# Stick-breaking decoder trunk: compression weights in another pool, and VectorE's branch-d chain in parts behind weight splits

## The chip, the cores and the metric

The kernel runs on one core of a Trainium2 chip. The metric is the device time of one execution in microseconds; smaller is better. Five engines work beside each other, each through its own instructions in their order: TensorE (PE, with its weight loads as PEld), VectorE (DVE), ScalarE (ACT), GpSimd (POOL) and SyncE (SP), which here issues nearly all DMA transfers.

## The reference

Two layers (DEPTH 2) of a trunk with four causal token mixers, for 512 tokens of width 1024, in float32. Each layer normalises x, projects it by one matrix `w_in`, mixes in four branches and merges them through per-channel gates:

```
h = rmsnorm(x, norm_g[l])
c = split_columns(h @ w_in[l])
y_a = dilated_window_attention(...)          # 3 patterns, ALiBi
y_b = mla_attention(...)                     # low-rank q and kv
y_c = nsa_attention(... w1, b1, w2, b2 ...)  # compressed blocks, selected blocks, window
y_d = stick_breaking_attention(...)
merged = sum_i sigmoid(h @ w_merge[l, i] + b_merge[l, i]) * ((y_i * silu(gate_i)) @ w_branch[l, i])
x = x + merged @ w_out[l]
```

The two pieces that the change touches are the compression of branch c and the chain of branch d:

```
# compression: 31 blocks of 32 tokens, two stacks (keys, values)
hid = gelu(blocks.reshape(B, n_cmp, NSA_CMP_BLOCK * Dk) @ w1 + b1)
return hid @ w2 + b2
# stick breaking, per head and 128 queries
log1m = where(mask, log_sigmoid(-z), 0)
after = cumsum(log1m, reverse=True) - log1m
a = where(mask, exp(log_sigmoid(z) + after), 0)
out = a @ v
```

## The kernel before

**Weight chunks.** Nearly all of TensorE's work is products of the activations with weight chunks of 128 columns (`[P, 8, P]`, 512 KB; merge chunks take 2 rows of blocks more, 640 KB). A product in full float32 precision is made of three matmuls of reduced precision on split operands, high times high, high times low and low times high (`mm3`, L189 to L191, each 128x512). `split_chunk` (L234) loads a chunk on SP's queue into a `stage` tile (3 buffers) and splits it into a high and a low tile of the pool `w5`, which has 4 buffers, so that two chunks fit. The split is shared: of the first 5 row blocks of 128 (`W_SHARE`) ScalarE makes the high half (L175) and VectorE the low one (L176); of the other 3 (5 in a merge chunk) GpSimd makes both (L100, L185). A matmul of L191 needs the low tile, one of L189 the high one.

**Order.** A scheduler of the language puts the instructions of all stages in order from a timeline of its own and from priorities. `tc.high_priority` lets branches A, D and C begin before the weight work that stands ahead of them in the code, so that TensorE has products to do while the vector engines work on an attention. `after(a, b, why)` (L310) lays a dependence: instruction b does not start before a is done.

**Around the change.** In each layer the tail of branch A runs beside the compression and merge chunk (0,1). A's pairs go in units of two heads: scores (L290), VectorE's sum with the bias (L300), ScalarE's exponential (L302), VectorE's reciprocal (L303), GpSimd's normalisation (L305), TensorE's transposes (L325), ScalarE's copy (L327), TensorE's product with v (L331). The compression (`compress`, L584) projects keys and values, takes four tiles of `w1` (512 KB each, `[P, 8, P]`) through `stage` tiles and makes eight small matmuls (L629) with each, then gelu (L636 to L651).

Branch d (L724 to L759) goes in two pairs of heads. A pair has scores (L737) less a mask (L738) in three parts: two x tiles of 128x1024 and one `su` tile of 128x512. Then the minimum with 30 (L740), ScalarE's exponential (L741) and logarithm (L744), and on VectorE, for each part, the maximum (L746), scans (L751) and a subtraction (L752), with ScalarE's exponential behind (L753); then transposes and products with v. The chunks that are multiplied beside pair 0 are merge chunks, then the two chunks of `c_q` (`q_chunk`; low tiles w_448 and w_453); beside pair 1 those of the merge, of `c_gate` (`gate_chunks`, whose last step on VectorE is L568) and of the next merge. Layer 1 repeats layer 0, 545 us later. Line numbers are those of the kernel before.

Of the kernel before, what the change touches and what calls it, by code (L numbers as in the profile page):

```python
# [10 lines left out]
F32 = mybir.dt.float32  # L11
F32R = mybir.dt.float32r
AF = mybir.ActivationFunctionType
OP = mybir.AluOpType
PSUM = bass.MemoryType.PSUM

P = 128
# [28 lines left out]
W_SHARE = 5  # L46
# [40 lines left out]
def hybrid_trunk(ctx: ExitStack, tc: tile.TileContext, x, norm_g, w_in, mla_q_norm, mla_w_uq, mla_kv_norm,  # L87
# [3 lines left out]
    V, A, G, T = nc.vector, nc.scalar, nc.gpsimd, nc.tensor  # L91
# [16 lines left out]
    def s4(shape, dt=F32):  # L108
        return mk(sb, shape, dt, "s4", N_S4)
# [22 lines left out]
    def stage(shape):  # L132
        return mk(wp, shape, F32, "stage", 3)
# [38 lines left out]
    def split(hi, lo, src, scale=None):  # L172

        if scale is None:
            A.activation(hi, src, AF.Copy)  # L175
            V.tensor_tensor(lo, src, hi.bitcast(F32), op=OP.subtract)  # L176
        else:
            A.activation(hi, src, AF.Copy, scale=scale)
            V.scalar_tensor_tensor(lo, src, scale, hi.bitcast(F32), op0=OP.mult, op1=OP.subtract)

    def shared_split(hi, lo, src, a):

        split(hi[:, :a], lo[:, :a], src[:, :a])
        pool_copy(hi[:, a:], src[:, a:])
        G.tensor_tensor(lo[:, a:], src[:, a:], hi[:, a:].bitcast(F32), op=OP.subtract)  # L185

    def mm3(acc, sh, sl, mh, ml, start, stop):

# [42 lines left out]
    def wview(w, r0, rows, c0, cols):  # L231
        return w[r0:r0 + rows, c0:c0 + cols].rearrange("(k p) c -> p k c", p=P)

    def split_chunk(parts, nk):  # L234

        st = stage([P, nk, P])
        for k0, k1, c0, c1, ap in parts:
            nc.sync.dma_start(st[:, k0:k1, c0:c1], ap)
        hi, lo = w5([P, nk, P], F32R), w5([P, nk, P], F32R)
        shared_split(hi, lo, st, W_SHARE)  # L240
        return hi, lo

    def in_chunk(l, c0):
# [127 lines left out]
    def merge_chunks(l, plan, ys, am, mT):  # L371
        for cp, i in plan:
            first = cp not in am
            if first:
                am[cp] = [s4([P, 2, S]), 0]
            acc, am[cp][1] = am[cp][0], am[cp][1] + 1
            last = am[cp][1] == 4
            if last:
                mT[cp] = [(x4 if cp < 2 else s4)([P, 2, S], F32R) for _ in range(2)]
            for j in range(2):  # L380
                c = 2 * cp + j
                w = split_chunk([(0, KD, 0, P, wview(w_merge[l, i], 0, D, P * c, P)),
                                 (KD, KD + 2, 0, P, wview(w_branch[l, i], 0, 256, P * c, P))], KD + 2)
                pg = ps_d()
                proj_T(w, pg)
                th = th_tile()
                A.activation(th, pg, AF.Tanh, scale=0.5, bias=bmT[l][:, 8 * i + c:8 * i + c + 1])  # L387
                pb = ps_d()
                for k in range(2):
                    mm3(pb, w[0][:, KD + k], w[1][:, KD + k], ys[i][0][:, k], ys[i][1][:, k], k == 0, k == 1)  # L390
                if first:
                    V.scalar_tensor_tensor(acc[:, j], th, 1.0, pb, op0=OP.add, op1=OP.mult)
                else:
                    V.scalar_tensor_tensor(th, th, 1.0, pb, op0=OP.add, op1=OP.mult)  # L394
                    G.tensor_tensor(acc[:, j], acc[:, j], th, op=OP.add)  # L395
                if last:
                    split(mT[cp][0][:, j], mT[cp][1][:, j], acc[:, j], scale=0.5)
# [45 lines left out]
    for l in range(DEPTH):  # L443
# [140 lines left out]
        def compress():  # L584
# [37 lines left out]
            acc = ps_d()  # L622
            for s_ in range(2):
                for hf in range(2):
                    w1 = stage([P, 8, P])
                    nc.sync.dma_start(w1, nsa_w1[l, s_, 1024 * hf:1024 * hf + 1024].rearrange("(q p) c -> p q c", p=P))
                    for q in range(8 * hf, 8 * hf + 8):
                        g = 32 * (q % 4)
                        T.matmul(acc[g:g + 32, s_ * P:(s_ + 1) * P], blocks[s_][:, q], w1[:, q % 8], start=q < 4,  # L629
                                 stop=q >= 12, skip_group_check=True)  # L630
# [76 lines left out]
        merge_chunks(l, ((0, 1),), y, am, mT)  # L707
        gd = gate_chunks("d_gate")
        ks, kw, kc, vbd = compress()
        merge_chunks(l, ((1, 0),), y, am, mT)  # L710
        c_q = [q_chunk("c_q", c, cscale[:, c:c + 1]) for c in range(2)]

# [3 lines left out]
        cgv = cg.rearrange("p t (h j) -> p t h j", j=3)  # L716

        mark_c = tc.cur_priority
        merge_chunks(l, ((1, 1),), y, am, mT)
        gc = gate_chunks("c_gate")  # L720
        merge_chunks(l, ((0, 0),), y, am, mT)
# [2 lines left out]
        with tc.high_priority(offset=tc.cur_priority - mark):  # L724
            y[3] = new_y()
            for pr in range(2):
                ze = [(x4([P, 2, 512]), x4([P, 2, 512]), unit_tile().rearrange("p (h c) -> p h c", h=2)) for _ in range(2)]
                place = ((1, 384, 512), (2, 0, 256), (1, 0, 384), (0, 0, 512))

                def part(i, qt, h):  # L730
                    j, c0, c1 = place[qt]
                    return ze[i][j][:, h, c0:c1]

                for qt in (3, 2, 0, 1):
                    w = (qt + 1) * P
                    for h in range(2):
                        s = qk_unit(stacked(d_q[pr], d_k[pr][h], h), qt, w)  # L737
                        V.tensor_tensor(part(0, qt, h), s[:, :w], mask_tab[:, S + 1 - w:], op=OP.subtract)  # L738
                for j in range(3):
                    V.tensor_scalar(ze[1][j], ze[0][j], 30.0, None, op0=OP.min)  # L740
                    ex = A.activation(ze[1][j], ze[1][j], AF.Exp)  # L741
                with tc.issue_after(ex.ins):
                    for j in range(3):
                        A.activation(ze[1][j], ze[1][j], AF.Ln, bias=1.0)  # L744
                for j in range(3):
                    V.tensor_tensor(ze[1][j], ze[0][j], ze[1][j], op=OP.max)  # L746
                    for qt in range(NT):
                        if place[qt][0] == j:
                            for h in range(2):
                                er = part(1, qt, h)[:, ::-1]  # L750
                                V.tensor_tensor_scan(er, er, er, 0.0, op0=OP.add, op1=OP.bypass)  # L751
                    V.tensor_tensor(ze[0][j], ze[0][j], ze[1][j], op=OP.subtract)  # L752
                    A.activation(ze[0][j], ze[0][j], AF.Exp)  # L753
                acc = ps_o()
                for qts in ((3,), (2,), (0, 1)):
                    pv_cluster([([part(0, qt, h) for h in range(2)], qt,
                                 lambda h, kb: v_ad[1][:, kb, (2 * pr + h) * 64:(2 * pr + h + 1) * 64], False, True)
                                for qt in qts], acc)
                d_done = finish_pair(acc, gd, y[3], pr)  # L759
# [129 lines left out]
```

## Time and profile before

| | us |
|---|---|
| median of 3 runs | 1110.68 (1110.3 to 1111.24) |
| the profiled execution | 1114.14 |
| its span | 1112.4 |
| TensorE busy | 1078.8 (97%) |
| TensorE weight loads busy | 861.7 (77%) |
| VectorE, ScalarE, GpSimd busy | 541.5, 441.2, 464.4 |

Busy times are over the span. In the profile, a group line gives count, busy time and mean, and behind the last bar the idle time of the engine ahead of its instructions with what ended it. A timeline line gives start, duration, engine, line, operation, destination and sources, count, and in brackets the idle time before. A line with x12 is twelve instructions in a row. Matmuls overlap in the pipe, so the distance of two starts tells more than a duration. For the small matmuls (L331, L629) the trace has two records for each one of the program.

### The profile page before, as it was taken

To read this page: it belongs to the slowest core of one execution; us is meant where nothing else is said; L and a number is where in the kernel's file an instruction comes from. 1 tells how busy PE (TensorE), PEld (TensorE's weight loads), DVE (VectorE), ACT (ScalarE), POOL (GpSimd) and SP (SyncE) were. 2 spreads that over 40 slices of the span, in tenths; PEclk is the share of its full clock that TensorE was granted. 3 is DMA by queue.
4 is the path that set the end of the run, shared out by engine and by line. 5 is a ranking of instruction groups with operands and counts; after the bars stand their busy time and mean duration, and the time that the engine had idled before them with its cause. 6 is when DMAs were issued, how large, how long until landed. Compare 5 with 4: busy or idle time off the path is not lost.

```text
span 1112.4 us, 15422 instructions
## 1 busy us (share of the span) xinstructions
PE 1078.8 (97%) x5652; PEld 861.7 (77%) x5652; DVE 541.5 (49%) x1008; ACT 441.2 (40%) x894; POOL 464.4 (42%) x506
## 2 busy tenths in 40 slices
PE   8999999979999999999999999999799999999997
PEld 5888787758678878787888887777577787878876
DVE  6435444485835344234453546445955544532342
ACT  5424444344434434223243344435453343432232
POOL 5243354333436466452011544324334464656421
PEclk9999999989999999999999999999899999999999
DMA  7422232522232221435413322225223222233322
GB/s 245 103 57 76 76 105 58 162 66 72 71 91 75 71 73 48 133 93 153 121 57 96 95 74 70 76 77 166 62 71 94 72 71 72 72 92 90 117 77 76
DMA packets 161677, 100.87 MB, mean 91 GB/s; under 512 B 14913, under 2 KB 151489, under 8 KB 161602
## 3 DMA queue, kind: packets, MB, share of 16 engines
q1 hardware_dynamic: 160880, 98.75, 30.9%
q10 hardware_dynamic: 722, 1.14, 0.3%
q8 instruction: 45, 0.74, 0.3%
q14 instruction: 30, 0.25, 0.1%
HBM read 95.67 MB, written 4.19 MB: 90 GB/s over the span
## 4 chain that ended last, share of the span: by engine, by line
PE 83%; DVE 7%; DMA 4%; ACT 2%; issue 2%; POOL 1%; SPq 0%; POOLq 0%; DVEq 0%; ACTq 0%
PE pd L191 22%; PE pd L189 22%; PE pd L190 22%; PE po L331 5%; PE pss L290 5%; PE pt L325 4%; DMA stage<-in_w_out_dram 4%; DVE x L751 2%; DVE w L176 1%; ACT y L175 1%; DVE x L746 1%; DMA x<-in_x_dram 1%; PE pd L629 0%; PE pt L678 0%; DVE x L752 0%
## 5 line engine op out<-in xcount | busy, mean ns | idle before, releaser
L191 PE MATMUL pd<-hT,w 128*128 128x512 f32 x832 | 333.2, 401 | 11.2 <-DVE w L176 11.2
L189 PE MATMUL pd<-hT,w 128*128 128x512 f32 x832 | 335.0, 403 | 7.8 <-ACT w L175 4.7
L190 PE MATMUL pd<-hT,w 128*128 128x512 f32 x832 | 334.2, 402 | 0.0
L100 POOL TENSOR_SCALAR w<-stage 128x640 fp32r<-128x640 f32 (+1 forms) x104 | 78.1, 751 | 297.8 <-PE pd L190 192.3
L191 PEld LDWEIGHTS pd<-hT,w 128*128 128x128 f32 x832 | 157.8, 190 | 48.4 <-DVE w L176 13.6
L189 PEld LDWEIGHTS pd<-hT,w 128*128 128x128 f32 x832 | 157.8, 190 | 44.5 <-ACT w L175 6.2
L176 DVE TENSOR_TENSOR w<-stage,w 128x640 fp32r<-128x640 f32 (+2 forms) x116 | 157.5, 1357 | 69.7 <-ACT w L175 57.1
L190 PEld LDWEIGHTS pd<-hT,w 128*128 128x128 f32 x832 | 157.8, 190 | 33.6 <-issue 0.7
L185 POOL TENSOR_TENSOR w<-stage,w 128x640 fp32r<-128x640 f32 (+1 forms) x104 | 161.7, 1555 | 49.7 <-PE pd L190 39.8
L175 ACT ACTIVATE w<-stage 128x640 fp32r<-128x640 f32 (+2 forms) x116 | 87.5, 759 | 105.9 <-PE pd L190 65.8
L302 ACT ACTIVATE su<-su,stat 128x128 f32<-128x128 f32 (+3 forms) x128 | 71.2, 557 | 76.4 <-DVE stat L300 75.9
L395 POOL TENSOR_TENSOR s<-s,th 128x512 f32<-128x512 f32 x48 | 77.9, 1623 | 31.7 <-DVE th L394 31.7
L327 ACT ACTIVATE pt<-pt 128x384 f32<-128x384 f32 (+2 forms) x120 | 57.6, 521 | 77.3 <-PE pt L325 77.1
L394 DVE SCALAR_TENSOR_TENSOR th<-th,pd 128x512 f32<-128x512 f32 x48 | 32.9, 686 | 110.5 <-PE pd L191 95.2
L387 ACT ACTIVATE th<-pd,bmT 128x512 f32<-128x512 f32 x64 | 43.9, 685 | 74.6 <-PE pd L191 74.5
L305 POOL TENSOR_SCALAR su<-su,stat 128x128 f32<-128x128 f32 (+3 forms) x64 | 36.7, 579 | 79.2 <-DVE stat L303 78.1
L325 PE MATMUL pt<-small,su 128*128 128x128 f32 x336 | 60.4, 280 | 0.0
L307 POOL TENSOR_SCALAR su<-su,stat,cg 128x128 f32<-128x128 f32 (+3 forms) x64 | 41.0, 647 | 43.1 <-DVE stat L303 42.9
L189 PE MATMUL pd<-y,w 128*128 128x512 f32 x128 | 51.0, 401 | 1.9 <-ACT th L387 1.7
L325 PEld LDWEIGHTS pt<-small,su 128*128 128x128 f32 x336 | 40.2, 140 | 15.6 <-issue 8.5
L191 PE MATMUL pd<-y,w 128*128 128x512 f32 x128 | 50.5, 394 | 0.0
L190 PE MATMUL pd<-y,w 128*128 128x512 f32 x128 | 50.5, 394 | 0.0
(239 smaller groups left out, 1582.5 us busy)
## 6 DMA issues: line engine op xcount, KB each, us to landing
stage<-in_w_merge_dram SPq DMA_DIRECT2D x64, 512.0 KB, 3.9
stage<-in_w_in_dram SPq DMA_DIRECT2D x38, 512.0 KB, 3.9
stage<-in_w_branch_dram SPq DMA_DIRECT2D x64, 128.0 KB, 3.8
stage<-in_w_out_dram SPq DMA_DIRECT2D x16, 512.0 KB, 3.9
stage<-in_w_in_dram SPq DMA_DIRECT2D x20, 256.0 KB, 3.2
stage<-in_nsa_w_dram SPq DMA_DIRECT2D x8, 512.0 KB, 4.0
stage<-in_w_in_dram SPq DMA_DIRECT2D x8, 352.0 KB, 4.6
x<-in_tab_a_dram SPq DMA_DIRECT2D x4, 512.0 KB, 4.2
```

The lines of the kernel that those rows point to most:

```text
L100: G.tensor_scalar(o, i, 1.0, 1.0, op0=OP.mult, op1=OP.mult)
L175: A.activation(hi, src, AF.Copy)
L176: V.tensor_tensor(lo, src, hi.bitcast(F32), op=OP.subtract)
L185: G.tensor_tensor(lo[:, a:], src[:, a:], hi[:, a:].bitcast(F32), op=OP.subtract)
L189: T.matmul(acc, sh, mh, start=start, stop=False)
L190: T.matmul(acc, sh, ml, start=False, stop=False)
L191: T.matmul(acc, sl, mh, start=False, stop=stop)
L290: T.matmul(s[:, :width], q[:, qt * P:(qt + 1) * P], k[:, :width], start=i == 0, stop=i == len(passes) - 1)
L302: A.activation(e[:, :width], e[:, :width], AF.Exp, scale=-1.0, bias=st[:, 0:1], accum_out=st[:, 1:2])
L325: T.transpose(pt[:, i], u[0][h][:, kb * P:(kb + 1) * P], ident)
L327: ready = A.activation(pT[:, :n], pt[:, :n], AF.Copy)
L395: G.tensor_tensor(acc[:, j], acc[:, j], th, op=OP.add)
```

## The change

The compression's `w1` tiles come from the pool `s4` (11 buffers) and no more from `stage`. `split_chunk` keeps VectorE's instruction of each split in a list, `w_split`. In branch d the maximum of the first part of a pair (j = 0), and that of the second (j = 1), each wait for the split of one chunk: in pair 0 those of the two `c_q` chunks (w_448, w_453), in pair 1 those of the second `c_gate` chunk and of the first chunk of merge (0,0). The third part (`su`) waits for none.

```diff
     def shared_split(hi, lo, src, a):
-        split(hi[:, :a], lo[:, :a], src[:, :a])
+        done = split(hi[:, :a], lo[:, :a], src[:, :a])
         pool_copy(hi[:, a:], src[:, a:])
         G.tensor_tensor(lo[:, a:], src[:, a:], hi[:, a:].bitcast(F32), op=OP.subtract)
+        return done
...
+    w_split = []
...
         hi, lo = w5([P, nk, P], F32R), w5([P, nk, P], F32R)
-        shared_split(hi, lo, st, W_SHARE)
+        w_split.append(shared_split(hi, lo, st, W_SHARE))
...
-                    w1 = stage([P, 8, P])
+                    w1 = s4([P, 8, P])
...
         ks, kw, kc, vbd = compress()
+        n_10 = len(w_split)
         merge_chunks(l, ((1, 0),), y, am, mT)
...
         mark_c = tc.cur_priority
+        n_11 = len(w_split)
...
                 for j in range(3):
-                    V.tensor_tensor(ze[1][j], ze[0][j], ze[1][j], op=OP.max)
+                    larger = V.tensor_tensor(ze[1][j], ze[0][j], ze[1][j], op=OP.max)
+                    if j < 2:
+
+                        after(w_split[(n_10 + 2, n_11 + 3)[pr] + j], larger, "weights first")
```

`split` itself now returns VectorE's instruction, else it is as it was. The change adds eight lines ahead of branch d: L746, L751, L752 of before are L750, L758, L759 after, L290, L325, L331 are L292, L327, L333, L392 is L394, L568 is L570, L629 is L631 and L636 is L638.

On VectorE, pair 0 of branch d in layer 0: x_496 and x_497 are the two x parts, su_2565 the third, w_448 and w_453 the low tiles of `c_q`. Before:

```order
L746 TENSOR_TENSOR x_496_2563<-x_493_2560,x_496_2563 128x1024
L746 TENSOR_TENSOR x_497_2564<-x_494_2561,x_497_2564 128x1024
L392 SCALAR_TENSOR_TENSOR s_432_2137<-th_2172,pd_2174 128x512
L751 SCALAR_TENSOR_TENSOR x_496_2563<-x_496_2563 128x512 x2
L746 TENSOR_TENSOR su_2565<-su_2562,su_2565 128x512
L644 TENSOR_SCALAR gelu_2116<-gelu_2116 128x64
L751 SCALAR_TENSOR_TENSOR x_497_2564<-x_497_2564 128x128 x2
L751 SCALAR_TENSOR_TENSOR x_497_2564<-x_497_2564 128x384 x2
L176 TENSOR_TENSOR w_448_2230<-stage_2227,w_447_2229 128x640
L392 SCALAR_TENSOR_TENSOR s_432_2137<-th_2216,pd_2218 128x512
L176 TENSOR_TENSOR w_453_2268<-stage_2265,w_452_2267 128x640
```

The same place after the change, from the split of w_448 to the first scans of x_497:

```order
L176 TENSOR_TENSOR w_448_2230<-stage_2227,w_447_2229 128x640
L750 TENSOR_TENSOR x_496_2563<-x_493_2560,x_496_2563 128x1024
L758 SCALAR_TENSOR_TENSOR x_496_2563<-x_496_2563 128x512 x2
L759 TENSOR_TENSOR x_493_2560<-x_493_2560,x_496_2563 128x1024
L638 TENSOR_SCALAR hid_2067<-pt_2111,b_401_1966 128x32
L742 TENSOR_TENSOR x_521_2687<-pss_2693,mask_tab 128x512
L742 TENSOR_TENSOR x_521_2687<-pss_2697,mask_tab 128x512
L642 TENSOR_TENSOR gelu_2116<-hid_2067 128x64
L394 SCALAR_TENSOR_TENSOR s_432_2137<-th_2216,pd_2218 128x512
L643 TENSOR_SCALAR gelu_2116<-gelu_2116 128x64
L644 TENSOR_TENSOR gelu_2116<-gelu_2116,hid_2067 128x64
L176 TENSOR_TENSOR w_453_2268<-stage_2265,w_452_2267 128x640
```

Ahead of the split of w_448 now stands the third part alone (maximum, scans and subtraction of su_2565); the first x part has moved behind it, and the second behind the split of w_453.

On TensorE, A's last units and the w1 matmuls (pd_2068), before: pss_17xx are scores of A, pt and po its transposes and products with v, pss_25xx scores of pair 0 of d.

```order
L629 MATMUL pd_2068<-stage_2079,s_410_2011 32x128 x2
L290 MATMUL pss_1724<-y_297_1524,y_292_1486 128x384 x2
L290 MATMUL pss_1733<-y_298_1528,y_292_1486 128x384 x2
L629 MATMUL pd_2068<-stage_2079,s_410_2011 32x128 x4
L629 MATMUL pd_2068<-stage_2089,s_411_2017 32x128 x4
L325 MATMUL pt_1706<-small,su_1691 128x128 x2
L629 MATMUL pd_2068<-stage_2089,s_411_2017 32x128 x3
L325 MATMUL pt_1712<-small,su_1700 128x128 x2
L629 MATMUL pd_2068<-stage_2089,s_411_2017 32x128
L290 MATMUL pss_1760<-y_297_1524,y_292_1486 128x512 x2
L290 MATMUL pss_1769<-y_298_1528,y_292_1486 128x512 x2
L629 MATMUL pd_2068<-stage_2099,s_411_2017 32x128 x8
```

After, the end of that stretch (su_1772 is A's last unit, pss_2693 and pss_2697 the first scores of pair 1):

```order
L327 MATMUL pt_1785<-small,su_1772 128x128 x4
L292 MATMUL pss_2582<-s_157_858,s_152_820 128x128 x2
L292 MATMUL pss_2586<-s_158_862,s_152_820 128x128 x2
L292 MATMUL pss_2590<-s_157_858,s_152_820 128x256 x2
L292 MATMUL pss_2594<-s_158_862,s_152_820 128x256 x2
L333 MATMUL po_1669<-pt_1783,s_107_497 64x128
L333 MATMUL po_1669<-pt_1790,s_107_497 64x128
...
L292 MATMUL pss_2693<-s_168_937,s_163_899 128x512 x2
L292 MATMUL pss_2697<-s_169_941,s_163_899 128x512 x2
L631 MATMUL pd_2068<-s_420_2069,s_410_2011 32x128 x8
L189 MATMUL pd_2147<-hT_75,w_434_2141 128x512
```

The w1 matmuls have left A's tail: eight stand here, and 24 behind 22 products of the merge chunk (pd_2147). From pss_1769 to the transposes pt_1785 TensorE has eight transposes, four score units (pss_2566 to pss_2578) and twelve products with v, and no product with a weight chunk; in the order before, the products of pd_2147 begin behind pss_2570.

On SP's queue, the last of the four w1 loads before (stage_2099), and the chunks behind it: stage_2138 and stage_2182 are merge (1,0), stage_2227 and stage_2265 `c_q`, stage_2305 the first chunk of merge (1,1).

```order
L626 DMA stage_2099<-in_nsa_w_dram 128x8x128
L238 DMA stage_2138<-in_w_merge_dram 128x8x128
L238 DMA stage_2138<-in_w_branch_dram 128x2x128
L238 DMA stage_2182<-in_w_merge_dram 128x8x128
L238 DMA stage_2182<-in_w_branch_dram 128x2x128
L238 DMA stage_2227<-in_w_in_dram 128x8x128
```

After, five chunks go ahead of them:

```order
L240 DMA stage_2227<-in_w_in_dram 128x8x128
L240 DMA stage_2265<-in_w_in_dram 128x8x128
L240 DMA stage_2305<-in_w_merge_dram 128x8x128
L240 DMA stage_2305<-in_w_branch_dram 128x2x128
L628 DMA s_420_2069<-in_nsa_w_dram 128x8x128
L628 DMA s_421_2079<-in_nsa_w_dram 128x8x128
```

The four w1 loads now wait for buffers of `s4`: the first for the score unit pss_2594, the second for A's last product with v, the third for VectorE's last step of A's accumulation (L339), the fourth for the eight matmuls of the first.

## Rows read from the trace of the kernel before

**Rows 1.** TensorE's waits in the whole run: releaser, us, times, longest.

```profile
PE pd L191 <- DVE w L176: 11.2, 4, 4.8
PE pd L189 <- ACT w L175: 4.7, 2, 2.3
PE pd L189 <- DVE s L568: 2.9, 2, 1.7
```

**Rows 2.** Timeline of TensorE, 231 to 250 us.

```profile
234.74 0.39 PE L191 MATMUL pd<-y,w 128*128 128x512 f32 x1
237.46 0.50 PE L189 MATMUL pd<-hT,w 128*128 128x512 f32 x1 [2.33 <-ACT w L175]
...
243.60 0.80 PE L191 MATMUL pd<-hT,w 128*128 128x512 f32 x1 [4.62 <-DVE w L176]
...
248.83 0.39 PE L191 MATMUL pd<-hT,w 128*128 128x512 f32 x1
249.06 0.40 PE L189 MATMUL pd<-hT,w 128*128 128x512 f32 x1
```

**Rows 3.** Timeline of VectorE, 232 to 245 us.

```profile
233.06 2.67 DVE L746 TENSOR_TENSOR x<-x,x 128x1024 f32<-128x1024 f32 x2 [2.03 <-ACT x L744]
...
242.75 0.79 DVE L176 TENSOR_TENSOR w<-stage,w 128x640 fp32r<-128x640 f32 x1
```

**Rows 4.** Windows of 1 to 2 us: busy times, then TensorE's granted clock.

```profile
244.00:246.00 2.00, 2.00 (x6) 1.52 (x6) 2.00 (x4) 0.00 (x0) 0.00 (x0) 0.50 0.54 157
...
249.00:250.00 1.00, 1.00 (x6) 0.77 (x6) 1.00 (x3) 0.55 (x1) 0.00 (x0) 1.00 0.30 91
...
12.00:14.00 2.00, 1.21 (x7) 0.69 (x6) 2.00 (x2) 1.88 (x7) 1.82 (x3) 1.00 1.04 354
```

**Rows 5.** Timeline of TensorE, 203 to 217 us.

```profile
206.42 0.41 PE L629 MATMUL pd<-stage,s 128*32 128x128 f32 x2
206.75 0.33 PE L325 MATMUL pt<-small,su 128*128 128x128 f32 x1
...
211.37 0.65 PE L629 MATMUL pd<-stage,s 128*32 128x128 f32 x16
211.95 0.55 PE L325 MATMUL pt<-small,su 128*128 128x128 f32 x3
...
213.53 1.17 PE L290 MATMUL pss<-s,s 128*128 128x512 f32 x4
```

**Rows 6.** Lines with forms apart, 199 to 310 us: busy time, mean ns.

```profile
L331 PE MATMUL po<-pt,s 128*64 128x128 f32 x96 | 7.2, 281 | 0.0
...
L305 POOL TENSOR_SCALAR su<-su,stat 128x512 f32<-128x512 f32 x2 | 2.0, 982 | 0.0
...
L302 ACT ACTIVATE su<-su,stat 128x512 f32<-128x512 f32 x2 | 1.4, 717 | 1.1 <-DVE stat L300 1.1
...
L300 DVE CUSTOM_DVE_ANT_0 su<-pss,x 128x512 f32<-128x512 f32 x2 | 1.3, 688 | 1.0 <-PE pss L290 1.0
```

**Rows 7.** Timeline of GpSimd, 211 to 217 us.

```profile
213.19 0.72 POOL L100 TENSOR_SCALAR w<-stage 128x640 fp32r<-128x640 f32 x1 [2.34 <-DMA stage<-in_w_branch_dram]
...
215.12 1.57 POOL L185 TENSOR_TENSOR w<-stage,w 128x640 fp32r<-128x640 f32 x1
```

**Rows 8.** Timeline of VectorE, 249 to 253.5 us.

```profile
252.03 2.21 DVE L176 TENSOR_TENSOR w<-stage,w 128x640 fp32r<-128x640 f32 x1 [1.65 <-ACT w L175]
```

**Rows 9.** DMA issues of the w1 tiles: count, KB, median us to landing.

```profile
stage<-in_nsa_w_dram SPq DMA_DIRECT2D x8, 512.0 KB, 4.0
```

**Rows 10.** Lines with forms apart: VectorE's subtraction in branch d.

```profile
L752 DVE TENSOR_TENSOR x<-x,x 128x1024 f32<-128x1024 f32 x4 | 4.8, 1208 | 0.0
```

**Rows 11.** Timeline of TensorE, 290 to 302.5 us.

```profile
291.69 0.50 PE L191 MATMUL pd<-hT,w 128*128 128x512 f32 x1 [0.89 <-DVE w L176]
...
301.28 0.50 PE L189 MATMUL pd<-hT,w 128*128 128x512 f32 x1 [1.73 <-DVE s L568]
```

**Rows 12.** Timeline of VectorE, 282.5 to 302 us.

```profile
300.55 0.67 DVE L568 SCALAR_TENSOR_TENSOR s<-th,pd 128x512 f32<-128x512 f32 x1
```

More of the change, by code (lines that the diff above doesn't have):

```diff
@@ L175, in split @@
             A.activation(hi, src, AF.Copy)
[L176 to L179, printed above, removed]
+            return V.tensor_tensor(lo, src, hi.bitcast(F32), op=OP.subtract)
+        A.activation(hi, src, AF.Copy, scale=scale)
+        return V.scalar_tensor_tensor(lo, src, scale, hi.bitcast(F32), op0=OP.mult, op1=OP.subtract)
     def shared_split(hi, lo, src, a):
-        split(hi[:, :a], lo[:, :a], src[:, :a])
+        done = split(hi[:, :a], lo[:, :a], src[:, :a])
         pool_copy(hi[:, a:], src[:, a:])
         G.tensor_tensor(lo[:, a:], src[:, a:], hi[:, a:].bitcast(F32), op=OP.subtract)
+        return done
     def mm3(acc, sh, sl, mh, ml, start, stop):
```

## Prediction

> **What bounds the kernel now.** I read the page first: TensorE is busy 97% of the span, so only what it waits for, and what it does slowly, can be won. Next its waits, grouped by releaser [rows 1]. Three groups belong to the stretch that the change touches: low halves of weights from VectorE's L176 (11.2 us in four waits), high halves from ScalarE (4.7 in two) and L568 (2.9 in two). Each has an even number of waits, one half in each layer, so I work out layer 0 and double it.
>
> The timeline of TensorE then shows where they lie [rows 2]. In pair 0 of branch d it stops at the first chunk of c_q: 2.33 us for the high half, four matmuls, and 4.62 us for the low half. Look in that row at the releaser, then go to that engine's timeline [rows 3]: VectorE starts the two maxima of d at 233.06 and comes to the split of w_448 only at 242.75. For 9.7 us it did work of branch d that TensorE did not need yet. That is the cause of the 4.62; the 2.33 is the same lateness one step ahead, since the weight buffers turn over in order.
>
> The stall leaves a second price. Between the starts at 243.60 and 248.83 lie twelve matmul distances in 5.23 us, 0.436 each, against 0.23 from 248.83 to 249.06 [rows 2]. The windows say why: a granted clock of 0.50 (the 1.2 GHz level) at 244 to 246 us, and 1.00 (2.4 GHz) again at 249 to 250 [rows 4]. Twelve at full rate take 2.8, so 2.4 us are lost. Together pair 0 costs 2.33 + 4.62 + 2.4 = 9.35 us per layer.
>
> In pair 1 the same shape is small: 0.89 us for a low half and 1.73 us for L568 [rows 11], 2.6 together, the second because VectorE comes to that L568 at 300.55 [rows 12].
>
> **The change part by part.** *The waits in pair 0's chain.* They put the first x part of d behind the split of w_448 and the second behind w_453. I ask first whether both splits then come in time. The four buffers of split halves hold two chunks. Call T the moment when merge chunk pd_2174 is finished: the buffers of w_448 come free then. TensorE has 31 more matmuls before it needs them (the chunk pd_2191 and its product with y), 31 x 0.23 = 7.1 us. ScalarE's half and VectorE's half (0.79 us alone [rows 3], 2.21 us beside GpSimd's half [rows 8]) take some 3 us. So w_448 is in time with 4 us to spare. Then VectorE does the first x part: maximum and scans, about half of the 9.7 us stretch (4.9), its subtraction 1.2 [rows 10], two masks and the merge's step at some 0.7 each, and five small operations, under 1 together: about 9 us. The split of w_453 ends near T + 3 + 9 + 0.8 = T + 12.8. TensorE needs it after the 24 matmuls of the first c_q chunk and two score units (6.5 us), near T + 14. It is in time by 1 us or so, the thinnest margin here. I take all 9.35 as removed.
>
> Queued behind each waiting maximum on VectorE are that part's scans and subtraction, then ScalarE's exponential and the transposes. These are later by the length of two splits, some 2 to 4 us; what covers it is the second c_q chunk's product (5.6 us). If the cover is gone, the transposes of d come late by as much.
>
> *The w1 matmuls.* Before, they run in seven pieces between A's transposes and scores. Two small ones take 0.33 from start to start, sixteen take 0.58 [rows 5]: about 0.018 each and 0.29 for a piece. After, there are two pieces: five fewer, 1.5 us less work on TensorE.
>
> *What is lost in A's tail.* Without w1 and pd_2147 as filling, TensorE has, between the scores of A's last unit and its transposes, only four score units (1.0 us for the four records at 213.53, so twice that), twelve transposes (about 0.5 for three [rows 5]) and 24 records of products with v (7.2 / 96 each [rows 6]): 2.0 + 2.0 + 1.8 = 5.8 us. The chain of that unit is two bias sums of 0.69, an exponential of 0.72 and a normalisation of 0.98 [rows 6], 3.1 us. In front of the normalisation GpSimd now has the two pieces of a merge chunk's split, 0.72 and 1.57 us [rows 7], and in front of VectorE's steps a split of 0.79 to 2.21. That is 6.2 to 7.6 us, thus a wait of 0.4 to 1.8. For the reciprocal and the signals between engines I lean up and take **1.3 us**. Bounds: 0, if the splits are done earlier, and 4.1, if GpSimd's two pieces of the second chunk (2.3) stand there too.
>
> *The w1 loads.* The first now leaves only when TensorE has finished the score unit pss_2594. A w1 load takes 4.0 us from issue to landing [rows 9]. Until its matmuls TensorE has eight products with v (sixteen records, 1.2 us [rows 6]) and two score units (1.0 [rows 5]). With 0.2 us for the release and issue, the wait is 4.0 + 0.2 - 2.2 = **2.0 us**. The other loads run behind 22 products of 0.23 us (5.1 us); the fourth, which starts after the first tile's own eight matmuls, lands 1 us ahead of them. Bounds: 0, if the wait in A's tail already covers it, and 4.0, if the load itself has 6 us, as when it shares the engines with the five chunks now ahead of it on SP's queue.
>
> *Pair 1.* I cost its two waits at no gain. VectorE has the same steps between the logarithm's end and the second L568 in both orders; only their order differs, so L568 comes as late as at 300.55 [rows 12]. The 0.89 wait for a low half goes, and TensorE arrives at L568 that much sooner. What it waits there, 1.73 before, becomes about 2.6. If L568 is no longer last, up to 2.6 us would be won.
>
> *Sum.* Per layer 9.35 + 1.5 - 1.3 - 2.0 = 7.55 us, 15.1 in both. The profiled execution of 1114.1 would be 1099. It stood 3.4 above the median of the runs, so for runs 1110.7 - 15.1 = **1096 us**.
>
> **A rule weighed against the trace.** TensorE works sparsely in A's tail after the change, in bursts with waits between, with no weight chunk to fill them. Rows of both kinds exist. The clock was 0.50 at 244 to 246 us, behind a wait of 4.62; at 12 to 14 us it stayed at 1.00 although TensorE was busy only 1.21 of 2 us [rows 4]. The waits that I expect, 1.3 and 2.0, are nearer to the second. The Trainium skill ("TensorE: Matmul & The Clock Gate", section "HAM oscillation — how this bites in real kernels") tells of a kernel whose bursts of matmuls are parted by waits for transfers and each start at the low clock. By that rule the w1 wait would bring the 2.4 us back in each layer and the sum would be 1101; by the 12 to 14 us row it stays 1096.
>
> **The rivals.**
> - *Full relief.* The wait in A's tail is nothing, and pair 1's 2.6 us go as well. For it: VectorE is idle in places of the tail, and the splits may be done before the scores. Against: L568's chain has no fewer steps. Per layer 7.55 + 1.3 + 2.6 = 11.45, so 1088 us.
> - *The clock falls in A's tail.* A stretch of 5.2 us at half rate, as at 243.60, costs 2.4 us per layer: 1096 + 4.8 = 1101 us. For it stands the 0.50 behind a wait; against it the 12 to 14 us window.
> - *The stall only moves.* The split of w_453 is late: it has 1 us of margin. If GpSimd's and VectorE's halves go at the 2.21 rate and the first x part is slowed alike, w_453 comes 3 to 4 us late and A's tail takes its 4.1. Then 9.35 + 1.5 - 4.1 - 2.0 - 3.5 leaves about 1 us per layer: 1108.5 to 1113 us, no change.
> - *Slower: the w1 load stops TensorE.* TensorE takes its matmuls in order, so everything waits behind the first w1 tile. SP's queue is in order too: the w1 loads stand behind five chunks, whose stage buffers come free only as the splits are done. Two merge splits late on GpSimd (2.3 each) and two loads of about 4 us behind one another make the wait some 12 us in place of 2.0. It decides from 7.55 us more than I took; at 10 more per layer the time is 1116 us. Against it: the splits of both chunks stand early in VectorE's order, and a load is far shorter than A's tail.
>
> **How the numbers follow.** A measurement of this kernel tells about 0.2% (2.2 us) from no change. The forecast has 0.56: a cause that is seen in the rows, and prices with bounds of a few us. Its own range, by the bounds of the three disputed terms, is 1092 to 1101. Full relief 0.14, the clock 0.12, the stall that moves 0.09, slower 0.09. The first three are faster: 0.82; the fourth is the same, 0.09; the last slower, 0.09. The range of 1087 to 1106 holds the first three and leaves out the last two.
>
> **What would show it.** Right: in pair 0 no wait of TensorE over 1 us for L176 or L175 at c_q, and a clock of 1.00 there; on VectorE the split of w_448 ahead of the first maximum of an x part; two pieces of w1 matmuls, the first behind a wait of about 2 us for its load; a wait of about 1.3 us for the normalisation or the copy in A's tail; in pair 1 one wait of about 2.6 us for L568. Wrong: a wait at w_453, a first w1 wait over 5 us, a clock of 0.50 near A's end, or late transposes of d behind the second c_q chunk.

## The result, and the profile after

The changed kernel takes 1096.84 us, median of 4 runs (1095.93 to 1097.09), against 1110.49 for the kernel before (1109.84 to 1111.24): a ratio of 0.9875, 95% interval 0.9858 to 0.9892. The predicted time was 1096. Its profiled execution has a span of 1093.9 us, 18.5 less than the one before; in the runs the gain is 13.65 us, mostly since the profiled execution before stood 3.65 us above the median of those runs and the one after 0.9 below its own.

The waits of TensorE in the whole run, which answer to [rows 1] (releaser, us, times, longest):

```profile
PE pd L189 <- DVE s L570: 4.6, 2, 2.3
PE pss L292 <- DVE su L742: 2.8, 2, 1.6
PE pt L327 <- POOL su L307: 2.7, 4, 1.2
...
PE pd L631 <- DMA s<-in_nsa_w_dram: 1.3, 2, 0.8
```

The two groups for halves of weights, 11.2 and 4.7 us before, are gone. At c_q there is no wait, and the windows that answer to [rows 4] show TensorE busy all the time at the full clock (behind the two ends of the stretch: its length, then busy times of TensorE, its loads, VectorE, ScalarE, GpSimd; then the granted clock):

```profile
239.00:241.00 2.00, 2.00 (x11) 1.64 (x10) 1.97 (x6) 0.26 (x1) 0.00 (x0) 1.00 0.00 0
...
244.00:246.00 2.00, 2.00 (x11) 1.64 (x10) 1.90 (x3) 0.78 (x2) 1.92 (x2) 1.00 0.00 0
```

On VectorE's timeline, which answers to [rows 3], each split of c_q stands ahead of an x part:

```profile
226.34 0.69 DVE L759 TENSOR_TENSOR su<-su,su 128x512 f32<-128x512 f32 x1
229.66 0.69 DVE L394 SCALAR_TENSOR_TENSOR s<-th,pd 128x512 f32<-128x512 f32 x1 [2.63 <-PE pd L191]
...
230.43 1.35 DVE L176 TENSOR_TENSOR w<-stage,w 128x640 fp32r<-128x640 f32 x1
231.81 1.23 DVE L750 TENSOR_TENSOR x<-x,x 128x1024 f32<-128x1024 f32 x1
...
239.42 0.82 DVE L176 TENSOR_TENSOR w<-stage,w 128x640 fp32r<-128x640 f32 x1
```

The row at 229.66 was not foreseen: VectorE stood idle for 2.63 us there, and the x parts, whose logarithm had long ended, were held back meanwhile. TensorE's timeline of A's tail and of pair 1:

```profile
208.88 0.44 PE L327 MATMUL pt<-small,su 128*128 128x128 f32 x2 [1.19 <-POOL su L307]
...
215.11 0.73 PE L292 MATMUL pss<-s,s 128*128 128x256 f32 x4 [0.16 <-DVE x L742]
...
218.43 1.20 PE L292 MATMUL pss<-s,s 128*128 128x512 f32 x4 [1.56 <-DVE su L742]
220.12 0.64 PE L631 MATMUL pd<-s,s 128*32 128x128 f32 x16 [0.50 <-DMA s<-in_nsa_w_dram]
...
292.23 0.50 PE L189 MATMUL pd<-hT,w 128*128 128x512 f32 x1 [2.32 <-DVE s L570]
```

The last score unit of d's pair 0, both its heads, starts at 215.11 and ends at 215.84. Before, the second head's half stood behind weight products and ended at 228.22:

```profile
227.82 0.40 PE L290 MATMUL pss<-s,s 128*128 128x256 f32 x2
```

These scores come 12.4 us earlier, and the chain of branch d can start earlier with them. The experiments tell whether that, or the waits, removed the stall.

### The profile page after: what moved, and what is told of

Read it like the earlier page. It is cut to its first block, busy times and chain, and to the rows that moved or that the text cites. A ratio compares the mean times of both kernels' runs of the same rounds, so it can differ in the third digit from the quotient of the medians.

```text
span 1093.9 us, 15435 instructions
## 1 busy us (share of the span) xinstructions
PE 1069.6 (98%) x5652; PEld 859.2 (79%) x5652; DVE 542.2 (50%) x1008; ACT 439.6 (40%) x894; POOL 457.6 (42%) x506
## 4 chain that ended last, share of the span: by engine, by line
PE 86%; DMA 5%; DVE 4%; issue 2%; ACT 1%; POOL 1%; SPq 0%; POOLq 0%; DVEq 0%; ACTq 0%
PE pd L189 23%; PE pd L190 23%; PE pd L191 23%; PE po L333 5%; PE pss L292 5%; PE pt L327 4%; DMA stage<-in_w_out_dram 4%; ACT y L175 1%; DMA s<-in_nsa_w_dram 1%; DVE x L758 1%; POOL w L184 1%; DVE w L176 1%; DVE su L758 0%; DVE x L750 0%; PE pt L680 0%
## 5 line engine op out<-in xcount | busy, mean ns | idle before, releaser
L100 POOL TENSOR_SCALAR w<-stage 128x640 fp32r<-128x640 f32 (+1 forms) x104 | 72.0, 692 | 309.1 <-PE pd L190 204.7
L184 POOL TENSOR_TENSOR w<-stage,w 128x640 fp32r<-128x640 f32 (+1 forms) x104 | 158.9, 1528 | 51.2 <-PE pd L190 39.7
L397 POOL TENSOR_TENSOR s<-s,th 128x512 f32<-128x512 f32 x48 | 81.3, 1694 | 35.2 <-DVE th L396 35.2
L327 PE MATMUL pt<-small,su 128*128 128x128 f32 x336 | 60.0, 279 | 2.7 <-POOL su L307 2.7
L309 POOL TENSOR_SCALAR su<-su,stat,cg 128x128 f32<-128x128 f32 (+3 forms) x64 | 38.5, 607 | 39.3 <-DVE stat L305 39.1
L327 PEld LDWEIGHTS pt<-small,su 128*128 128x128 f32 x336 | 40.2, 140 | 18.0 <-issue 6.5
L302 DVE CUSTOM_DVE_ANT_0 su<-pss,dist_tab 128x128 f32<-128x128 f32 (+3 forms) x64 | 29.3, 486 | 47.3 <-PE pss L292 38.5
L189 PE MATMUL pd<-y,w 128*128 128x512 f32 x128 | 50.5, 397 | 1.3 <-ACT th L389 1.3
L190 PE MATMUL pd<-y,w 128*128 128x512 f32 x128 | 50.6, 395 | 0.0
```

Of the source, the lines that this page charges most:

```text
L100: G.tensor_scalar(o, i, 1.0, 1.0, op0=OP.mult, op1=OP.mult)
L189: T.matmul(acc, sh, mh, start=start, stop=False)
L190: T.matmul(acc, sh, ml, start=False, stop=False)
L327: T.transpose(pt[:, i], u[0][h][:, kb * P:(kb + 1) * P], ident)
```

## The experiments

Theory 1 is the prediction's: the waits laid in VectorE's chain remove the stall at c_q, and the w1 move only costs a little. Theory 2: the w1 move does it, and the waits matter little. Times of a kernel are compared with those of the kernel before on the same chip (1111.7 to 1112.0 us there).

### One part alone

Only the pool (e1_pool):

```diff
-                    if j < 2:
-
-                        after(w_split[(n_10 + 2, n_11 + 3)[pr] + j], larger, "weights first")
```

> Only the w1 tiles move to the other pool; branch d's chain waits for no split. Theory 1 (the prediction's): the waits in the chain remove the stall at c_q, and the w1 move only costs some 3.6 us of waits in A's tail and at the load and gives back 1.3 us of pieces per layer. Then the stall of 9.35 us per layer stands as before: about 1110.5 + 2 x 2.3 = 1115 us. Theory 2: the w1 move itself does most of it, since without the w1 pieces and the merge chunk in A's tail the scores of d's pair 0 are done some 9 us earlier (the first maximum at 224.3 us in the changed kernel, at 233.06 before), so that the chain is nearly over when the c_q weights come. Then 1098 to 1103 us, with a wait of 1 to 3 us left at the first c_q chunk and the clock at 1.00.

Measured: 1097.78 us, ratio 0.9879 (0.9863 to 0.9896). Within the measurement that is the whole gain, without a single wait in the chain. It lies just below the range of theory 2, since the wait of 1 to 3 us that was still expected at c_q is not there.

Only the waits (e2_waits):

```diff
-                    w1 = s4([P, 8, P])
+                    w1 = stage([P, 8, P])
```

> Only the waits in branch d's chain; the w1 tiles stay in the stage buffers. Theory 1: the stall at c_q goes and A's tail keeps its filling, so there is no wait there: 1110.5 - 2 x 9.35 = about 1092 us. Theory 2: the chain still starts at 233 us and now waits for two splits too, so its exponentials and transposes come some 3 to 4 us later than before and TensorE waits for them, or for the score buffers of pair 1, in place of the weights: 1100 to 1108 us.

Measured: 1112.08 us, ratio 1.0002 (0.9992 to 1.0011): nothing, 20 us above what theory 1 wanted and 4 above the upper end of theory 2. Theory 1 falls, at both ends.

With the waits in one pair only (e3_pair0, e4_pair1):

```diff
-                    if j < 2:
+                    if j < 2 and pr == 0:    # or pr == 1
```

> The whole change, but the waits only in pair 0 of branch d. Both theories: pair 1 goes back to a wait of 0.9 us for a low half and 1.7 us for L570, 2.6 in place of 2.3 per layer, so 1097 to 1098 us, the same as the whole change within the measurement. If the waits of pair 1 carry a part of the gain, it is 1100 us or more.

> The whole change, but the waits only in pair 1 of branch d. It should come out as the w1 move alone, within 1 us: theory 1 about 1115 us, theory 2 1098 to 1103 us.

Measured: 1097.48 us, ratio 0.9873 (0.9856 to 0.9889), and 1098.16 us, ratio 0.9880 (0.9866 to 0.9895). All four kernels with w1 in `s4` lie within 1.4 us.

Why the pool alone is enough is on VectorE's timeline of e1_pool. Here L755 and L756 are the scans and the subtractions:

```profile
222.87 2.36 DVE L750 TENSOR_TENSOR x<-x,x 128x1024 f32<-128x1024 f32 x2 [2.47 <-ACT x L748]
...
236.16 0.68 DVE L756 TENSOR_TENSOR su<-su,su 128x512 f32<-128x512 f32 x1
...
237.51 0.82 DVE L176 TENSOR_TENSOR w<-stage,w 128x640 fp32r<-128x640 f32 x1
```

The maxima start at 222.87 and not at 233.06 [rows 3]. The whole chain of pair 0 is over at 236.8. The split of w_448 stands behind all of it, 14.6 us after the maxima began, and still comes in time: TensorE begins c_q at 238.21 and waits for no weight there.

Why the waits alone give nothing is on the timelines of e2_waits. First TensorE, where the 4.62 us for the low half [rows 2] are gone but the 2.33 for the high half are not:

```profile
236.79 0.50 PE L189 MATMUL pd<-hT,w 128*128 128x512 f32 x1 [2.33 <-ACT w L175]
...
239.09 0.63 PE L191 MATMUL pd<-hT,w 128*128 128x512 f32 x1
239.51 0.63 PE L189 MATMUL pd<-hT,w 128*128 128x512 f32 x1
```

then ScalarE, in the same kernel:

```profile
230.01 1.28 ACT L748 ACT_TABLE_LOAD   x1
231.30 2.01 ACT L748 ACTIVATE x<-x 128x1024 f32<-128x1024 f32 x2
233.22 0.62 ACT L748 ACTIVATE su<-su 128x512 f32<-128x512 f32 x1
233.85 1.28 ACT L645 ACT_TABLE_LOAD   x1
235.15 0.26 ACT L645 ACTIVATE gelu<-gelu 128x64 f32<-128x64 f32 x1
235.43 0.69 ACT L389 ACTIVATE th<-pd,bmT 128x512 f32<-128x512 f32 x1
236.01 1.35 ACT L175 ACTIVATE w<-stage 128x640 fp32r<-128x640 f32 x2
```

ScalarE is in order: the split of c_q stands behind a table load, three logarithms, another table load and two hyperbolic tangents without a gap between them. The high half was late because of branch d's logarithm, and the new order of VectorE's queue did not change that. Behind the stop the clock is still halved (0.43 from start to start at 239.09; granted clock 0.50 at 238 to 240 us). And the x parts, whose logarithm ends at the old time, are now held behind both splits: their maxima begin at 240.41, 7.3 us later than before, and in pair 1 TensorE waits 1.70 us for an exponential and 2.14 us for L570, with the clock at 0.50 behind them. What the low half gave, pair 1 took; in layer 1 a low half stops TensorE for 2.46 us besides, at 796.55.

### What the w1 move changes

Theory 3, formed here: what counts is where d's scores stand among the weight products. In `s4` the first w1 tile waits for a buffer that the score unit pss_2594 releases; in the order that comes out w1, and the merge products behind it, stand after these scores. The logarithm ends earlier, on ScalarE and VectorE alike. Theory 4: the stage buffers that w1 no longer holds let the chunks be loaded and split earlier. Two other pools for w1 tell them apart (e11_x4, e10_y4), both without waits in the chain:

```diff
-                    w1 = s4([P, 8, P])
+                    w1 = x4([P, 8, P])       # or y4
```

> The w1 tiles leave the stage buffers, but for the pool of branch d's x parts, and no wait is laid in the chain. In the order that comes out the w1 matmuls run in A's tail as before, and the last score unit of d's pair 0 stands behind 39 products of weight chunks, as before (40), where the changed kernel has none. Theory 3 (what the first four runs suggest): the gain comes from these scores going ahead of the weight chunks, so that ScalarE's logarithm ends 10 us earlier; then this kernel keeps the stall at c_q: 1106 to 1114 us. Theory 4: the gain comes from the stage buffers that w1 no longer holds, so that chunks are loaded and split earlier: 1096 to 1100 us.

> The same with the pool of the y tiles, no wait in the chain. Here the last score unit of pair 0 stands behind 30 products (merge (1,0)'s first chunk) and ahead of the other 24, so half way. Theory 3: the logarithm ends 4 to 7 us earlier than before, the chain ends 3 to 5 us late for c_q, A's tail is full: 1100 to 1107 us. Theory 4: 1093 to 1097 us, the waits of A's tail gone as well.

Measured: 1110.96 us, ratio 0.9999 (0.9989 to 1.0009), and 1115.38 us, ratio 1.0029 (1.0016 to 1.0043). Theory 4 falls: free stage buffers alone do not bring the gain. (That they bring nothing at all is not shown, since the chain also starts later in e11_x4, at 236.96.) The first is as theory 3 said. The second was expected half way and is slower than before: its maxima start only at 233.28, although its scores end 2.1 us earlier than before. VectorE, in order behind steps of A and of the compression, takes the mask of that last unit only at

```profile
228.24 0.75 DVE L742 TENSOR_TENSOR su<-pss,mask_tab 128x256 f32<-128x256 f32 x2
```

and ScalarE's last exponential ahead of the logarithms starts at 230.24, against 230.03 before. So scores that come earlier are not enough: the chain starts when the mask and exponential behind them are through. TensorE's waits at c_q, first in e11_x4:

```profile
238.55 0.79 PE L189 MATMUL pd<-hT,w 128*128 128x512 f32 x1 [4.17 <-ACT w L175]
...
242.69 0.80 PE L189 MATMUL pd<-hT,w 128*128 128x512 f32 x1 [2.92 <-ACT w L175]
```

and in e10_y4, where the lateness of the same chain lands on the merge's step of VectorE, L394, which holds a product's buffer:

```profile
237.39 0.50 PE L189 MATMUL pd<-hT,w 128*128 128x512 f32 x1 [1.01 <-ACT w L175]
...
243.67 0.76 PE L189 MATMUL pd<-hT,w 128*128 128x512 f32 x1 [5.55 <-DVE s L394]
```

Then the scores were put first by a dependence of their own in the kernel before, with w1 in the stage buffers (e14_scores), with the waits as well (e15_both), and with those of pair 0 alone (e17_pair0):

```diff
+                if pr == 0:
+                    after(last_score[0], proj_first[n_p], "scores first")
```

Here `last_score` is the last score matmul of pair 0, `proj_first[n_p]` the first product of merge (1,0).

> The kernel before with one edit of its own: the first matmul of merge (1,0) waits for the last score of d's pair 0. The w1 tiles stay in the stage buffers, their loads and matmuls where they were, and no wait is laid in VectorE's chain. In the order that comes out no product of a weight chunk stands ahead of these scores any more (40 before). Theory 3, that the early scores are the cause: the logarithm ends some 8 us earlier, the stall at c_q goes, and 1095 to 1102 us come out, with short waits in A's tail that is now filled by the w1 matmuls alone. Rival: the place of the w1 tiles or the loads' order is needed as well, then 1107 to 1113 us.

> The same edit and the waits on the splits in both pairs, the w1 tiles in the stage buffers. Theory 3: the waits are worth little once the scores are early, so within 3 us of the run with the scores alone; theory 1 in a weaker form (the waits remove what is left of the stall): 4 us or more faster than that run.

> The same with the waits in pair 0 only. If pair 1's waits are worth nothing there either, the same time within 1.5 us as with both pairs; if they only move the wait from a low half to L570, as in the changed kernel, pair 1 shows 2.3 to 2.6 us of waits in both.

Measured: 1107.74 us, ratio 0.9968 (0.9955 to 0.9981); 1106.04, ratio 0.9947 (0.9929 to 0.9965); 1113.92, ratio 1.0017 (1.0006 to 1.0028). The first is faster than before, but by 4 us only. That lies in the range of the rival (1107 to 1113 us): the place of the w1 tiles is needed as well. Its timelines say why, VectorE's and TensorE's:

```profile
228.27 2.36 DVE L754 TENSOR_TENSOR x<-x,x 128x1024 f32<-128x1024 f32 x2 [1.92 <-ACT x L752]
...
238.84 1.61 DVE L176 TENSOR_TENSOR w<-stage,w 128x640 fp32r<-128x640 f32 x1
```

```profile
215.50 0.66 PE L330 MATMUL pt<-small,su 128*128 128x128 f32 x4 [0.68 <-ACT pt L332]
...
219.57 0.66 PE L330 MATMUL pt<-small,su 128*128 128x128 f32 x4 [1.54 <-POOL su L310]
...
237.83 0.47 PE L189 MATMUL pd<-hT,w 128*128 128x512 f32 x1 [0.36 <-DVE s L397]
...
240.51 0.80 PE L191 MATMUL pd<-hT,w 128*128 128x512 f32 x1 [1.99 <-DVE w L176]
```

With the w1 matmuls still in A's tail the scores come only half of the way, and the maxima start at 228.27. From there to the split of w_448 are 10.6 us (9.7 before). TensorE is at c_q at 237.5, 9.2 us after the maxima, so most of the stall is covered and 1.99 us are left, with the clock at 0.50 behind them. The rest of the gain goes elsewhere: 0.68 + 1.54 = 2.2 us of new waits in A's tail, and 3.2 us of waits in pair 1 (2.6 before). The order of the loads, the rival's other half, has no run of its own; the split of w_448 follows VectorE's work without a gap here, so a load did not hold it. The second kernel lies within 3 us of the first, as theory 3 said, the third does not.

| kernel | last score unit of pair 0 ends | maxima of x start | waits at c_q, us | time, us |
|---|---|---|---|---|
| before | 228.22 | 233.06 | 2.33, 4.62 | 1110.5 to 1112.0 |
| e11_x4 | 230.48 | 236.96 | 4.17, 2.92 | 1110.96 |
| e10_y4 | 226.12 | 233.28 | 1.01, 5.55, 0.59 | 1115.38 |
| e14_scores | 222.58 | 228.27 | 0.36, 1.99 | 1107.74 |
| e1_pool | 215.90 | 222.87 | none | 1097.78 |

The five kernels of the table lay no wait on the weights in the chain. The stalls go with the start of the maxima: 7.0 to 7.2 us in the three that start at 233 or later, 2.4 us at 228, none at 223. TensorE reaches c_q between 234.4 and 237.5 in those that stop there. So for pair 0 theory 3 stands in this form: an earlier start of the chain removes the stall, and the new pool brings it by the scores ahead of the weight products and w1 out of A's tail together. The two kernels with waits besides, e15_both and e17_pair0, have no stall at c_q, and show what the waits cost where TensorE has little else to multiply: in both it waits 3.0 us at 252 for the exponential of an x part that was held back. None of the theories expected that the waits of pair 1 make 8 us of difference there; in e17_pair0 pair 1's transposes wait 2.31 us at 284 and the clock is 0.50 from 285 to 290, in e15_both there is neither. I did not look for the reason behind it with a run of its own.

### What is left, tried on

Pair 1's waits one chunk later (e7_shift1), and the second x part behind L570 (e9_gate, where `gated` is the list of L570's instructions):

```diff
-  after(w_split[(n_10 + 2, n_11 + 3)[pr] + j], larger, "weights first")
+  after(w_split[(n_10 + 2, n_11 + 4)[pr] + j], larger, "weights first")                       # e7_shift1
+  after(gated[-1] if pr and j else w_split[(n_10 + 2, n_11 + 3)[pr] + j], larger, ...)        # e9_gate
```

> The whole change, with pair 1's two waits laid on the splits one chunk later (the first and second chunk of merge (0,0)). VectorE's second L570 then stands ahead of the second x part. In the changed kernel TensorE waits 2.3 us for that L570 in each layer, ScalarE's part of it done some 5 us before. If that wait is VectorE's order alone, it goes: 1096.8 - 4.6 = 1092 us. The rival: the x parts come later by as much and the wait moves to the transposes of pair 1: 1096 to 1097 us.

> The whole change, with pair 1's second x part waiting for the second L570 itself instead of a split; the first x part stays where it is. As for the kernel with shifted waits: 1092 us if the order of VectorE is all, 1096 to 1097 if the transposes of pair 1 wait instead. This one delays only one part, so where the two differ, the first part's lateness has a price.

Measured: 1095.80 us, ratio 0.9860 (0.9845 to 0.9874), and 1104.02, ratio 0.9933 (0.9916 to 0.9949). The wait for L570 goes in both, and the rival holds for e7_shift1: the wait comes back at pair 1's transposes, 2.13 us there, and its time is not to be told from the changed kernel's. In e9_gate it costs more:

```profile
288.70 0.82 DVE L176 TENSOR_TENSOR w<-stage,w 128x640 fp32r<-128x640 f32 x1 [1.33 <-ACT w L175]
...
291.94 3.67 DVE L759 TENSOR_TENSOR_SCAN x<-x 128x128 f32<-128x128 f32 x4
```

```profile
298.01 1.43 PE L328 MATMUL pt<-small,x 128*128 128x128 f32 x6 [4.26 <-ACT x L761]
```

VectorE stood idle for 1.33 us with the second x part ready behind the wait, the transposes came 4.26 us late, and the clock fell to 0.54 behind them.

Last, scores first and w1 behind the merge (e20_late_w1): the whole change, e14's dependence, and

```diff
             ks, kw = s4([P, 2, S], F32R), s4([P, 2, S], F32R)
 ...
+            merge_chunks(l, ((1, 0),), y, am, mT)
             hid = tiny([P, 2, 32], "hid", 1)
 ...
-        merge_chunks(l, ((1, 0),), y, am, mT)
```

> The whole change, and two more edits: the first matmul of merge (1,0) waits for the last score of d's pair 0, and the w1 part of the compression is written behind merge (1,0), so that its loads have some 15 us and its matmuls stand behind both merge chunks. In the order that comes out A's tail and pair 0's scores are as in the changed kernel, the merge products follow them at once (the first scores of pair 1 stand behind 36 of them), and both L570 stand ahead of pair 1's maxima. Theory 3 (early scores are the cause, the place of w1 only brings them about): the stall at c_q stays away although w1 no longer stands ahead of the merge, the two waits behind A's tail (1.56 us for a score buffer, 0.50 us for the w1 load) go, and the 2.3 us for L570 go: 1096.8 - 2 x 4.4 = 1088 us at best, 1090 to 1094 if pair 1's transposes now wait. Rival: c_q comes 2 us earlier for TensorE without w1 ahead of it, and the stall is back, 1100 us or more.

Measured: 1111.71 us, ratio 1.0004 (0.9995 to 1.0013). In pair 0 it does what was expected, and w1 ahead of the merge is not needed for it: no stall at c_q, and no wait of 1.56 or 0.50 us behind A's tail. The loss is in pair 1, which was not foreseen:

```profile
294.64 2.88 DVE L758 TENSOR_TENSOR x<-x,x 128x1024 f32<-128x1024 f32 x2 [2.48 <-ACT x L756]
...
307.42 0.79 DVE L176 TENSOR_TENSOR w<-stage,w 128x640 fp32r<-128x640 f32 x1
```

```profile
269.97 1.04 PE L332 MATMUL pt<-small,x 128*128 128x128 f32 x8
...
308.27 0.70 PE L191 MATMUL pd<-hT,w 128*128 128x512 f32 x1 [4.65 <-DVE w L176]
```

Pair 1's maxima start at 294.64, and at 275.49 in the changed kernel. The same picture as pair 0 before: a split behind 12.8 us of branch d, and a stop of 4.65 us. The late start does not come of pair 1's scores (the last unit runs at 252.82, at 252.09 in the changed kernel) but of pair 0's transposes. The exponentials that they read end at 247.1 us, and still TensorE's order has the first transposes only at 269.97, behind products of weight chunks; in the changed kernel they start at 250.04. Why the order came out so is left open. Pair 1's minimum writes a tile that the transposes release, on VectorE:

```profile
283.59 0.69 DVE L752 TENSOR_SCALAR x<-x 128x1024 f32<-128x1024 f32 x1 [1.88 <-PE pt L332]
```

## Why the prediction was right in time and wrong in cause

**What failed.** The step "I take all 9.35 as removed", under the waits in pair 0's chain: by the runs these waits gain no time by themselves (ratio 1.0002). What removed the stall is the part that I had put down as a cost of 1.8 us net, the w1 tiles' new pool (0.9879 alone), through the earlier start of d's chain: its maxima begin at 222.87 in place of 233.06. The order that I printed on TensorE showed it: all score units of pair 0 ahead of the first product of pd_2147. I read there only the filling that A's tail lost, and did not ask what the scores, 12.4 us earlier, would do to the chain behind them.

**The second step that failed** is "the 2.33 is the same lateness one step ahead, since the weight buffers turn over in order". It was ScalarE, in order behind the logarithm. [Rows 2] names ScalarE as the releaser, and I explained it by VectorE without reading ScalarE's timeline. In e2_waits the 2.33 stands unchanged where the 4.62 is gone. The price of the clock hangs on the 2.33 too. In the kernel before TensorE still multiplies when the clock falls, behind the wait of 2.33 and ahead of the one of 4.62 (granted clock 1.00 at 238.0 to 238.4, 0.67 at 238.4 to 238.7):

```profile
238.70:239.00 0.30, 0.28 (x1) 0.00 (x0) 0.30 (x2) 0.00 (x0) 0.30 (x1) 0.50 0.00 0
```

**The terms**, where the stretch is told apart, in layer 0:
- Stall and clock: 9.35 foreseen. From 237.46 to 248.83 [rows 2] sixteen distances took 11.37 us against 3.73 at 0.233, which with the 2.33 makes 9.97; the four matmuls between the two waits were slow as well.
- w1's pieces: 1.5 foreseen. The first piece takes 0.58 us to the next start and the other, at 226.02, 1.45, against 3.29 for the seven before: 1.3.
- A's tail: 1.3 foreseen, 1.35 for the normalisation (0.16 and 1.19), behind GpSimd's half of a split as argued, but at A's unit of 256 columns, two ahead of the last one. Another 0.16 is a wait for a score buffer, at 215.11. Between A's last scores and pt_1785 the trace has twelve transposes, as in the sum, not the eight named under the change.
- The w1 load: 2.0 foreseen. 1.56 + 0.50 = 2.06 us, but TensorE stood for the score buffer first, and only the rest for the load; the load began at 215.87, at the end of the score unit pss_2594, and would have held it until 220.1 in any case. The 0.2 us that I took for release and issue stands in no row.
- Pair 1: no gain foreseen, 2.6 turning into one wait for L570. It is 2.32, 0.3 less.

These make 9.97 + 1.3 - 1.35 - 0.16 - 2.06 + 0.3 = 8.0 us. The layer, from A's scores at 203.9 or 203.7 us to the first transposes of the next at 553.2 or 544.0, became 9.0 us shorter; the last 1.0 I can't place. The prediction's own range, 1092 to 1101, does not follow from its bounds: both waits at nothing give 1089, both at their upper bounds 1105.

**The rivals.** The clock did not fall in A's tail: from 216 to 218 us TensorE is busy 0.87 of 2 us and the granted clock is 1.00. The waits there, 1.2 and 1.6 us, left it so, while behind 4.26 us in e9_gate, and behind 2.33 us in the kernel before, it fell. The Trainium skill ("TensorE: Matmul & The Clock Gate", section "HAM oscillation — how this bites in real kernels") tells of bursts parted by waits for transfers, some 3 to 5 us each, that start at the low clock. The 4.26 us agree with it, the sparse work in A's tail did not come to that. Full relief did not come, since neither wait it asked for went. The stall that only moves did not come in the changed kernel; it is what e2_waits shows, and e9_gate and e20_late_w1 for pair 1.

That the time was met is luck as far as the cause goes: the sum has the same stall in it whichever edit removed it. The signs that I had named as right, no wait at c_q and the split of w_448 ahead of the x part, are there too, but they could not tell which of the two edits did it. Had the change been the waits alone, the same reasoning would have said 1092 and missed by 20 us.

## What to carry to other kernels

When a late split stops TensorE, look at when the chain ahead of it on the in-order engine began, not only at what stands in the queue: here, with the start 10 us earlier, a split behind the whole chain came in time, while a better order with the old start left the wait for the other half and moved the rest. The buffer that a tile waits for can set the order: the same w1 tiles in three pools gave three orders, at 1097.78, 1110.96 and 1115.38 us. After a change of pool, see which instructions have moved ahead of the one that waits. And price each part of a change by itself: the prices of two parts can both be wrong and their sum right.

## What the runs showed that was not expected

- A stop of TensorE can cost more than its length, and not by length alone. Behind 2.32 us (the changed kernel) and 2.13 us (e7_shift1) the granted clock stayed at 1.00; behind 1.99 us in e14_scores, with 0.36 us of wait and two matmuls just ahead, it was 0.50, the lower of the two levels, from 241 to 243 us; behind 1.49 us in pair 1 of the same kernel, with a wait of 0.66 us that ended 1.1 us ahead of it, it was 0.50 from 292 to 294 us; behind 2.33 us in e2_waits and before it was 0.50 as well.
- Laying a wait on an instruction of VectorE cost time even where the operand was ready: 2.63 us idle in the changed kernel, 1.33 us in e9_gate, and 3.0 us of waiting for late exponentials in e15_both.
